# mLSTM heads of a hybrid decoder layer: chunks of 256 tokens with three carried states instead of 512 with one, and lone diagonal blocks as unsplit fp32 products

## The chip, the core and the metric

The kernel runs on one core of a Trainium2 chip. The core has a matrix engine (TensorE, PE in the profile, with its weight loads PEld), a vector engine (VectorE, DVE), an activation engine (ScalarE, ACT), a general engine (GpSimd, POOL) and a queue engine that issues most of the transfers (SyncE, SP). Matmuls write to eight accumulation banks of 128 x 512 fp32 (PSUM); everything else lives in on-chip memory (SBUF) of 128 partitions or in device memory. The metric is device time in microseconds (us).

## The reference

One decoder layer on 1024 tokens of width 1024, all in fp32. After an RMSNorm one input projection feeds three groups: a matrix-memory LSTM (mLSTM, 4 heads of 256), dilated causal attention (8 heads of 64) and cross-attention into 256 memory tokens (4 heads of 128). Each group is gated, the outputs go through one output projection, and a last RMSNorm closes the layer. Only the mLSTM matters here. It is defined in chunks, with a state C, n and a running maximum m carried from chunk to chunk:

```python
bcum = jnp.cumsum(lf_c, axis=-1)
dlog = bcum[..., :, None] - bcum[..., None, :] + li_c[..., None, :]
dlog = jnp.where(causal, dlog, -jnp.inf)
a = bcum + m_prev[..., None]
m = jnp.maximum(a, jnp.max(dlog, axis=-1))
wts = jnp.exp(dlog - m[..., None]) * jnp.einsum('bhtd,bhsd->bhts', qt, kt)
inter = jnp.exp(a - m)
num = inter[..., None] * jnp.einsum('bhtd,bhde->bhte', qt, C) + \
    jnp.einsum('bhts,bhse->bhte', wts, vt)
den = inter * jnp.einsum('bhtd,bhd->bht', qt, n) + jnp.sum(wts, axis=-1)
h_out = num / jnp.maximum(jnp.abs(den), jnp.exp(-m))[..., None]
...
C = decay[..., None, None] * C + jnp.einsum('bhsd,bhse->bhde', g[..., None] * kt, vt)
n = decay[..., None] * n + jnp.einsum('bhs,bhsd->bhd', g, kt)
```

The result does not depend on the length of a chunk: a longer chunk has more products inside it (tokens against earlier tokens), a shorter one more products with the carried state and more state updates.

## The kernel before

Every fp32 matrix product is done as a sum of three products of a reduced type ("fp32r"). An operand x is split by the helper split (L81, L82) into a high part, copied by ScalarE, and a low part, the rest, which VectorE subtracts; then high x high, high x low and low x high are accumulated in one PSUM bank. A moving operand of this type is never given fewer than 256 columns, so a lone block of 128 is computed with a neighbour's columns that are not used. In one place, the attention's last block (L483), a lone block is instead multiplied as plain fp32, unsplit.

The work runs in stages: normalisation and first projections, cross-attention, dilated attention, the projections of the mLSTM input with its convolution (xm_block), the gates, and then the mLSTM heads. Weight blocks form one list, stream; fill(n) takes the next n pieces of it, until(name) goes on to a named block. A piece is a set of projection matmuls into one of two "pj" banks. These pieces are put between the steps of the heads: the numbers of HEAD_FILLS say how many. In the head stage they are the mLSTM's output gates (om) and three quarters of the output projection (out0 to out2); what is left runs after the last head. The last quarter, "last", multiplies the second half of the mLSTM output, normalises and stores.

The program text does not fix the order of instructions on an engine. A scheduler of the compiler sets it: it takes ready instructions by their place in the text, by its own estimate of times. Once set, each engine goes through its list strictly in order.

gates() (from L616) makes, on four partitions (one per head) and 1024 tokens, the running maximum mm, the sums of the log forget gates t0 (restarted at each chunk, L643) and from them uu = t0 - mm. It stacks four rows in stk: li - t0 (row 0), the weight of a key in the state at the chunk's end (row 32), the weight of the carried state for a query (row 64) and exp(-m) (row 96). Eight transposes (L656) turn them into columns, gcol. uu goes to device memory as u_d, from where each head reads its row into all partitions.

A unit is (h, c): head h, half c of 512 tokens, which before is one chunk. There are 8, in order, each with four blocks of 128 tokens. For a unit run, with fills between:
- head_weights: reads the row ub (L669), adds the causal mask to its diagonal blocks (ud, L671), splits the input, projects the queries (L686 to L688, the key projection is folded into them), and for each key block s makes the products with all queries from s on (L704 to L706), exps (L709, L711), the weighted product (L712) and its split. A bank of "s1" (three) holds the scores.
- head_values: for c = 0 it first sums the state over all four blocks: transposes (L731), weighted keys (L734, L735), products with the values into two "s1" banks (L739 to L741), split into ch and cl. Then for each query block b: for c = 1 the product with the state (L757 to L759), scaled on ScalarE (L761) into ci; the weighted values over the key blocks up to b (L766 to L768) into the one "po" bank; then normalisation sums (L771 to L776).
- head_out: denominators, head norm, gate and store of the unit before.

Tiles are named by tags, and a tag has a fixed number of buffers: "g" 13, "x4" 3 (the split values vh and vl take two), "t2k" 4, P0 to P7 and sw0, sw1 one each. A tile with a taken tag waits until the earlier one is read for the last time.

Of the kernel before, what the change touches and what calls it, by code (L numbers as in the profile page):

```python
# [20 lines left out]
P = 128  # L21
# [7 lines left out]
def hymba_kernel(ctx: ExitStack, tc: tile.TileContext, x, xt, memt, chv, w_all, w_out,  # L29
# [23 lines left out]
    def s1():  # L53
        return pst("s1", 3)
# [22 lines left out]
    def dram(name, shape):  # L77
        return dr.tile(shape, F32, name=name, tag=name)
# [534 lines left out]
    u_d = dram("u_d", [4, T])  # L613
    late = {}

    def gates():  # L616
# [32 lines left out]
        S.activation(stk[32:36, 0:512], stk[0:4, 0:512], AF.Exp, bias=uu[:, 511:512])  # L649
        S.activation(stk[64:68, 512:1024], uu[:, 512:1024], AF.Exp, bias=mm[:, 511:512])  # L650
        S.activation(stk[96:100, :], mm, AF.Exp, scale=-1.0)
        nc.sync.dma_start(u_d, uu)
        for half in range(2):
            o = tp()
            for i in range(4):
                PE.transpose(o[:, i * P:(i + 1) * P], stk[:, (4 * half + i) * P:(4 * half + i + 1) * P], ident)  # L656
            V.tensor_copy(gcol[:, 4 * half:4 * half + 4, :, :],
                          o.rearrange("p (s q c) -> p s q c", s=4, q=4)[:, :, :, 0:4])
# [4 lines left out]
    def head_weights(u):  # L663
# [17 lines left out]
        xh, xl, qh, ql = [g4(F32R).rearrange("p (d t) -> p d t", d=2) for _ in range(4)]  # L681
        for d in range(2):
            split(xh[:, d, :], xl[:, d, :], xc[2 * h + d][:, cs])
        for d in range(2):
# [4 lines left out]
            split(qh[:, d, :], ql[:, d, :], o)  # L689
        vh, vl = x4([P, 4, 258], F32R), x4([P, 4, 258], F32R)  # L690
# [4 lines left out]
        for s in range(4):  # L695
            n = (4 - s) * P
            sg = 4 * c + s
            o = s1()
            ss = slice(s * P, (s + 1) * P)
            t0 = min(s, 2) * P  # L700
            w0 = s * P - t0
            wd = 512 - t0
            for d in range(2):
                PE.matmul(o[:, :wd], xh[:, d, ss], qh[:, d, t0:], start=d == 0, stop=False)  # L704
                PE.matmul(o[:, :wd], xh[:, d, ss], ql[:, d, t0:], start=False, stop=False)
                PE.matmul(o[:, :wd], xl[:, d, ss], qh[:, d, t0:], start=False, stop=d == 1)  # L706
            e = t2k()
            bias = gcol[:, sg, 0, h:h + 1]
            S.activation(e[:, :P], ud[:, s, :], AF.Exp, bias=bias)  # L709
            if n > P:  # L710
                S.activation(e[:, P:n], ub[:, (s + 1) * P:512], AF.Exp, bias=bias)  # L711
            V.tensor_tensor(e[:, :n], o[:, w0:w0 + n], e[:, :n], op=MUL)  # L712
            wh = tagged(("pth", "P3", "P1", "P0")[s], [P, n], F32R, 2 if s == 0 else 1)
            wl = tagged(("ptl", "P2", "sw0", "sw1")[s], [P, n], F32R, 2 if s == 0 else 1)
            split(wh, wl, e[:, :n])
            wts.append((wh, wl))
        return qh, ql, vh, vl, wts

    def head_values(u, parts):
# [5 lines left out]
        nc.sync.dma_start(gt, om_d[h][c])  # L725
        if c == 0:
            cps = [s1(), s1()]
            for s in range(4):
                o = tp()
                for d in range(2):  # L730
                    PE.transpose(o[:, d * P:(d + 1) * P], xc[2 * h + d][:, s * P:(s + 1) * P], ident)  # L731
                gs = gcol[:, s, 1, h:h + 1]
                xg = tagged("P4" if s % 2 == 0 else "P7", [P, 2, 256], F32R)
                S.activation(xg[:, 0, :], o[:, :256], AF.Copy, scale=gs)  # L734
                V.scalar_tensor_tensor(xg[:, 1, :], o[:, :256], gs, xg[:, 0, :].bitcast(F32), op0=MUL, op1=SUB)  # L735
                for d in range(2):
                    od = cps[d][:, :258]
                    dsl = slice(d * P, (d + 1) * P)
                    PE.matmul(od, xg[:, 0, dsl], vh[:, s, :], start=s == 0, stop=False)  # L739
                    PE.matmul(od, xg[:, 0, dsl], vl[:, s, :], start=False, stop=False)  # L740
                    PE.matmul(od, xg[:, 1, dsl], vh[:, s, :], start=False, stop=s == 3)  # L741
            ch = tagged("P5", [P, 2, 258], F32R)
            cl = tagged("P6", [P, 2, 258], F32R)
            for d in range(2):
                split(ch[:, d, :], cl[:, d, :], cps[d][:, :258])
            cst["c", h] = (ch, cl)
# [3 lines left out]
        for b in range(4):  # L750
            bs = slice(b * P, (b + 1) * P)
            ci = None
            if c == 1:
# [6 lines left out]
                ci = tagged("P4" if b % 2 == 0 else "P7", [P, 258])  # L760
                S.activation(ci, o[:, :258], AF.Copy, scale=gcol[:, 4 + b, 2, h:h + 1])  # L761
            o = po()
            for s in range(b + 1):
                wh, wl = wts[s]
                w0 = (b - s) * P
                PE.matmul(o[:, :258], wh[:, w0:w0 + P], vh[:, s, :], start=s == 0, stop=False)  # L766
# [9 lines left out]
            V.bn_aggr(mv[:, b, :], st6[:, b, :])  # L776
        return gt, dens, mv
# [389 lines left out]
```

## Time and profile before

| what | value |
|---|---|
| median of 3 runs | 1048.72 us (1047.23 to 1049.53) |
| the profiled execution | 1047.84 us |
| its span in the profile | 1046.0 us |
| granted TensorE clock, mean | 0.997 of full |
| TensorE busy in the first 600 us | 591.85 us |
| TensorE busy from 690 to 985 us | 292.3 us |
| TensorE busy in the last 61 us | 51.58 us |

The profile page lists for each engine the time in which it had an instruction at work. TensorE's matmuls overlap one another, so its busy time tells whether it stood idle, and the distance between the starts of two matmuls tells what one costs. A row of a group reads: line, engine, operation, tile written and tiles read, shapes, count, then busy time and the mean of one in ns, then the engine's idle time just before, with what ended it. A row of the waits reads: who waited, for whom, total us, times, longest us. A row of the time order reads: start, duration, engine, line, operation, tiles, shapes, count.

### The profile page before, as it was taken

The page shows a single profiled execution, that of the slowest core. Times are in us where ns is not written, and L with a number is a line of the kernel's source. Part 1 is how long each engine was busy: PE and PEld are TensorE (multiplying, and loading weights), DVE is VectorE, ACT ScalarE, POOL GpSimd, SP SyncE. Part 2 cuts the span into 40 slices and gives each one's busy share as a digit, 9 for nine tenths or more (in the row PEclk, how much of TensorE's full clock was granted, in tenths as well). Part 3 has the DMA queues.
Part 4 walks back from the last instruction along what each step waited for, and adds up shares of the span by engine and source line. Part 5 has one row for each costly group of instructions (what it writes and reads, how often), then busy time and mean ns, then how long its engine had stood idle before and what let it go on. Part 6 is the DMA issues. An engine that isn't in the chain of part 4 may idle for free.

```text
span 1046.0 us, 17249 instructions
## 1 busy us (share of the span) xinstructions
PE 1022.9 (98%) x6512; PEld 915.4 (88%) x6512; DVE 684.5 (65%) x1459; ACT 447.7 (43%) x884; POOL 293.9 (28%) x305
## 2 busy tenths in 40 slices
PE   9999999999999999999999999999999999999996
PEld 6888888988889888778888879899999999999996
DVE  8475555537687777875558886835568786774375
ACT  3543533325565555654324454534445344330221
POOL 1440212346611344601000011412044243121352
PEclk9999999999999999999999999999999999999998
DMA  9832222232201131322124344535389446333322
GB/s 332 271 110 99 84 84 85 75 88 74 60 27 55 47 73 39 76 68 61 71 71 126 107 132 142 140 102 152 112 276 290 136 125 188 105 122 122 107 113 84
DMA packets 75283, 121.09 MB, mean 116 GB/s; under 512 B 6460, under 2 KB 45884, under 8 KB 75200
## 3 DMA queue, kind: packets, MB, share of 16 engines
q1 hardware_dynamic: 60736, 105.83, 31.1%
q0 software_dynamic: 14464, 14.16, 6.2%
q8 instruction: 51, 0.84, 0.3%
q14 instruction: 32, 0.26, 0.1%
HBM read 83.22 MB, written 31.51 MB: 110 GB/s over the span
## 4 chain that ended last, share of the span: by engine, by line
PE 74%; DMA 9%; DVE 8%; issue 3%; ACT 2%; POOL 2%; SPq 0%; POOLq 0%; ACTq 0%; DVEq 0%
PE pj L167 11%; PE pj L168 11%; PE pj L169 11%; PE pj L178 4%; PE pj L179 4%; PE pj L177 4%; PE pj L211 3%; PE pj L212 3%; PE pj L213 3%; PE tp L478 3%; DMA wr<-in_w_out_dram 2%; DMA wr<-y 2%; PE s L453 2%; PE po L487 1%; PE s L454 1%
## 5 line engine op out<-in xcount | busy, mean ns | idle before, releaser
L167 PE MATMUL pj<-hn,wh 128*128 128x512 f32 x544 | 216.7, 398 | 3.3 <-DVE t2k L290 1.4
L169 PE MATMUL pj<-hn,wl 128*128 128x512 f32 x544 | 217.2, 400 | 0.0
L168 PE MATMUL pj<-hn,wh 128*128 128x512 f32 x544 | 216.2, 397 | 0.0
L167 PEld LDWEIGHTS pj<-hn,wh 128*128 128x128 f32 x544 | 102.3, 188 | 26.7 <-ACT t2k L383 1.7
L81 ACT ACTIVATE wh<-wr 128x1024 fp32r<-128x1024 f32 x67 | 70.8, 1058 | 127.3 <-PE pj L168 55.7
L169 PEld LDWEIGHTS pj<-hn,wl 128*128 128x128 f32 x544 | 102.2, 188 | 22.6
L168 PEld LDWEIGHTS pj<-hn,wh 128*128 128x128 f32 x544 | 102.3, 188 | 22.4
L211 PE MATMUL pj<-wh,hn 128*128 128x256 f32 x384 | 108.0, 281 | 0.5 <-ACT st L261 0.5
L213 PE MATMUL pj<-wh,hn 128*128 128x256 f32 x384 | 107.4, 280 | 0.0
L212 PE MATMUL pj<-wl,hn 128*128 128x256 f32 x384 | 107.3, 279 | 0.0
L82 POOL TENSOR_TENSOR wl<-wr,wh 128x1024 fp32r<-128x1024 f32 x23 | 55.8, 2426 | 137.9 <-ACT wh L81 98.9
L82 DVE TENSOR_TENSOR wl<-wr,wh 128x1024 fp32r<-128x1024 f32 x44 | 58.1, 1319 | 49.3 <-ACT wh L81 38.4
L81 ACT ACTIVATE pth<-tp 128x512 fp32r<-128x512 f32 (+2 forms) x96 | 50.2, 540 | 73.6 <-PE tp L478 42.5
L82 DVE TENSOR_TENSOR ptl<-tp,pth 128x512 fp32r<-128x512 f32 (+2 forms) x96 | 58.0, 618 | 28.6 <-ACT pth L81 28.2
L211 PEld LDWEIGHTS pj<-wh,hn 128*128 128x128 f32 x384 | 72.1, 188 | 1.4 <-ACT st L261 0.8
L212 PEld LDWEIGHTS pj<-wl,hn 128*128 128x128 f32 x384 | 72.1, 188 | 0.4
L213 PEld LDWEIGHTS pj<-wh,hn 128*128 128x128 f32 x384 | 72.0, 188 | 0.2
L177 PE MATMUL pj<-wh,hn 128*128 128x256 f32 x256 | 71.9, 281 | 0.0
L179 PE MATMUL pj<-wh,hn 128*128 128x256 f32 x256 | 71.6, 280 | 0.0
L178 PE MATMUL pj<-wl,hn 128*128 128x256 f32 x256 | 71.6, 280 | 0.0
L461 ACT ACTIVATE P<-P,mx 128x128 f32<-128x128 f32 (+3 forms) x64 | 49.3, 772 | 21.0 <-DVE mx L457 20.7
L851 DVE TENSOR_TENSOR hn<-pj,hn 128x512 f32<-128x512 f32 x48 | 32.9, 687 | 35.5 <-PE pj L179 35.4
(324 smaller groups left out, 2633.7 us busy)
## 6 DMA issues: line engine op xcount, KB each, us to landing
wr<-in_w_all_dram SPq DMA_DIRECT2D x54, 512.0 KB
x<-v POOLq DMA_DIRECT2D x16, 512.0 KB, 5.4
wr<-in_w_out_dram SPq DMA_DIRECT2D x16, 512.0 KB
wr<-y SPq DMA_DIRECT2D x16, 512.0 KB
y<-t2k SPq DMA_DIRECT2D x24, 256.0 KB
v<-P SPq DMA_DIRECT2D x24, 256.0 KB
zm<-st SPq DMA_DIRECT2D x16, 256.0 KB
g<-g POOLq DMA_DIRECT2D x32, 128.0 KB, 2.7
```

What stands on the lines that cost most here:

```text
L81: S.activation(hi, src, AF.Copy)
L82: (eng_lo or V).tensor_tensor(lo, src, hi.bitcast(F32), op=SUB)
L167: PE.matmul(o, hi[:, ks], ah(k, cs), start=k == 0, stop=False)
L168: PE.matmul(o, hi[:, ks], al(k, cs), start=False, stop=False)
L169: PE.matmul(o, lo[:, ks], ah(k, cs), start=False, stop=k == KC - 1)
L177: PE.matmul(o, ah(k, cs), hi[:, ks], start=k == 0, stop=False)
L178: PE.matmul(o, ah(k, cs), lo[:, ks], start=False, stop=False)
L179: PE.matmul(o, al(k, cs), hi[:, ks], start=False, stop=k == nk - 1)
L211: PE.matmul(oi, hn_h(4 * kh + k, cs), hi[:, ks], start=kh == 0 and k == 0 and i == 0, stop=False)
L212: PE.matmul(oi, hn_h(4 * kh + k, cs), lo[:, ks], start=False, stop=False)
L213: PE.matmul(oi, hn_l(4 * kh + k, cs), hi[:, ks], start=False, stop=kh == 1 and k == 3 and i == 1)
L461: S.activation(pr, pr, AF.Exp, bias=mx, scale=-1.0, accum_out=ls)
```

## The change

The head's text goes from one chunk of 512 tokens to two of 256, so that a head has four chunks and three carried states (after chunks 0, 1 and 2); units, fills and the order of calls stay.

- gates: sums restart every 256 tokens; key weights and state weights are made for three chunk ends. Two decay factors (state weight at the last token of chunks 1 and 2) go by two small transfers each through device memory into all partitions.
- head_weights: for each of the two chunks in the half, the first key block is multiplied with both query blocks (256 columns) in split form. The second key block against its own query block is the lone diagonal one: it is multiplied as unsplit fp32, from xc and from a copy qf of the queries in fp32, which ScalarE makes from the bank. One bank holds both, one product and one split of 384 columns follow.
- state_sums and state_done: the state work is cut out into two functions, over two blocks per chunk. The full state is kept in fp32 (cf, tag P6), multiplied by the decay and added to by VectorE, and split into ch and cl (P4, P5).
- head_values: for c = 0 state 0 is made first and used for blocks 2 and 3, and state 1 is made at the end. For c = 1 the sums of state 2 are made first, blocks 0 and 1 use state 1, state 2 is finished ahead of block 2. Weighted values run over the key blocks of the chunk alone.

```diff
+    dec_d = [dram(f"dec{c}", [1, 4]) for c in range(2)]
...
-        for c in range(2):
-            cs = slice(c * 512, c * 512 + 512)
-            V.tensor_tensor_scan(t0[:, cs], one1.broadcast_to([4, 512]), ff[:, cs], 0.0, op0=MUL, op1=ADD)
+        for c in range(4):
+            cs = slice(c * 256, c * 256 + 256)
+            V.tensor_tensor_scan(t0[:, cs], one1.broadcast_to([4, 256]), ff[:, cs], 0.0, op0=MUL, op1=ADD)
...
-        S.activation(stk[32:36, 0:512], stk[0:4, 0:512], AF.Exp, bias=uu[:, 511:512])
-        S.activation(stk[64:68, 512:1024], uu[:, 512:1024], AF.Exp, bias=mm[:, 511:512])
+        for c in range(3):
+            cs, e = slice(c * 256, c * 256 + 256), c * 256 + 255
+            S.activation(stk[64:68, e + 1:e + 257], uu[:, e + 1:e + 257], AF.Exp, bias=mm[:, e:e + 1])
+            S.activation(stk[32:36, cs], stk[0:4, cs], AF.Exp, bias=uu[:, e:e + 1])
         S.activation(stk[96:100, :], mm, AF.Exp, scale=-1.0)
         nc.sync.dma_start(u_d, uu)
+        for c in range(2):
+            late["dec", c] = tagged("mx", [P, 4], F32, 2)
+            nc.sync.dma_start(dec_d[c].rearrange("o h -> h o"), stk[64:68, c * 256 + 511:c * 256 + 512])
+            nc.sync.dma_start(late["dec", c], dec_d[c].broadcast_to([P, 4]))
...
+        qf = tagged("sw1", [P, 2, 2, P])
...
             split(qh[:, d, :], ql[:, d, :], o)
+            S.activation(qf[:, d, :, :], o.rearrange("p (a b t) -> p a b t", a=2, b=2)[:, :, 1, :], AF.Copy)
...
-        for s in range(4):
...
+        for a in range(2):
+            sg = 4 * c + 2 * a
+            x0 = c * 512
+            s0, s1_ = slice(2 * a * P, (2 * a + 1) * P), slice((2 * a + 1) * P, (2 * a + 2) * P)
+            both = slice(2 * a * P, (2 * a + 2) * P)
             o = s1()
             for d in range(2):
-                PE.matmul(o[:, :wd], xh[:, d, ss], qh[:, d, t0:], start=d == 0, stop=False)
-                PE.matmul(o[:, :wd], xh[:, d, ss], ql[:, d, t0:], start=False, stop=False)
-                PE.matmul(o[:, :wd], xl[:, d, ss], qh[:, d, t0:], start=False, stop=d == 1)
+                PE.matmul(o[:, :256], xh[:, d, s0], qh[:, d, both], start=d == 0, stop=False)
+                PE.matmul(o[:, :256], xh[:, d, s0], ql[:, d, both], start=False, stop=False)
+                PE.matmul(o[:, :256], xl[:, d, s0], qh[:, d, both], start=False, stop=d == 1)
+            for d in range(2):
+                PE.matmul(o[:, 256:384], xc[2 * h + d][:, x0 + s1_.start:x0 + s1_.stop], qf[:, d, a, :],
+                          start=d == 0, stop=d == 1)
             e = t2k()
+            S.activation(e[:, :P], ud[:, 2 * a, :], AF.Exp, bias=gcol[:, sg, 0, h:h + 1])
+            S.activation(e[:, P:256], ub[:, s1_], AF.Exp, bias=gcol[:, sg, 0, h:h + 1])
+            S.activation(e[:, 256:384], ud[:, 2 * a + 1, :], AF.Exp, bias=gcol[:, sg + 1, 0, h:h + 1])
+            V.tensor_tensor(e[:, :384], o[:, :384], e[:, :384], op=MUL)
+            wh = tagged(("pth", "P2")[a], [P, 384], F32R, 2 - a)
+            wl = tagged(("ptl", "sw0")[a], [P, 384], F32R, 2 - a)
+            split(wh, wl, e[:, :384])
...
+    def state_sums(h, cc, vh, vl):
+        gcol = late["gcol"]
+        cps = [s1(), s1()]
+        for i in range(2):
...
+            xg = tagged("P3" if i == 0 else "P7", [P, 2, 256], F32R)
...
+    def state_done(h, cc, cps):
+        if cc == 0:
+            cst["f", h] = tagged("P6", [P, 2, 258])
+        cf = cst["f", h]
+        ch = tagged("P4", [P, 2, 258], F32R)
+        cl = tagged("P5", [P, 2, 258], F32R)
+        for d in range(2):
+            if cc == 0:
+                S.activation(cf[:, d, :], cps[d][:, :258], AF.Copy)
+            else:
+                V.scalar_tensor_tensor(cf[:, d, :], cf[:, d, :], late["dec", cc - 1][:, h:h + 1], cps[d][:, :258],
+                                       op0=MUL, op1=ADD)
+            split(ch[:, d, :], cl[:, d, :], cps[d][:, :258] if cc == 0 else cf[:, d, :])
...
         if c == 0:
+            state_done(h, 0, state_sums(h, 0, vh, vl))
+        else:
+            late_state = state_sums(h, 2, vh, vl)
...
         for b in range(4):
...
-            if c == 1:
+            a = b // 2
+            if b == 2 and late_state is not None:
+                state_done(h, 2, late_state)
+            if 2 * c + a > 0:
...
-                ci = tagged("P4" if b % 2 == 0 else "P7", [P, 258])
+                ci = tagged("P3" if b % 2 == 0 else "P7", [P, 258])
...
-            for s in range(b + 1):
+            for s in range(2 * a, b + 1):
...
+        if c == 0:
+            state_done(h, 1, state_sums(h, 1, vh, vl))
         return gt, dens, mv
```

More of the change, by code (lines that the diff above doesn't have):

```diff
@@ L716, in head_weights @@
+            S.activation(e[:, P:256], ub[:, s1_], AF.Exp, bias=gcol[:, sg, 0, h:h + 1])
[4 more added lines that the diff above has]
+            split(wh, wl, e[:, :384])
             wts.append((wh, wl))
         return qh, ql, vh, vl, wts
+    def state_sums(h, cc, vh, vl):
+        gcol = late["gcol"]
+        cps = [s1(), s1()]
+        for i in range(2):
+            sg = 2 * cc + i
+            s = sg % 4
+            o = tp()
+            for d in range(2):
+                PE.transpose(o[:, d * P:(d + 1) * P], xc[2 * h + d][:, sg * P:(sg + 1) * P], ident)
+            gs = gcol[:, sg, 1, h:h + 1]
+            xg = tagged("P3" if i == 0 else "P7", [P, 2, 256], F32R)
+            S.activation(xg[:, 0, :], o[:, :256], AF.Copy, scale=gs)
+            V.scalar_tensor_tensor(xg[:, 1, :], o[:, :256], gs, xg[:, 0, :].bitcast(F32), op0=MUL, op1=SUB)
+            for d in range(2):
+                od = cps[d][:, :258]
+                dsl = slice(d * P, (d + 1) * P)
+                PE.matmul(od, xg[:, 0, dsl], vh[:, s, :], start=i == 0, stop=False)
+                PE.matmul(od, xg[:, 0, dsl], vl[:, s, :], start=False, stop=False)
+                PE.matmul(od, xg[:, 1, dsl], vh[:, s, :], start=False, stop=i == 1)
+        return cps
@@ new lines, in state_done @@
+    def state_done(h, cc, cps):
[4 more added lines that the diff above has]
+        cl = tagged("P5", [P, 2, 258], F32R)
+        for d in range(2):
+            if cc == 0:
[4 more added lines that the diff above has]
+            split(ch[:, d, :], cl[:, d, :], cps[d][:, :258] if cc == 0 else cf[:, d, :])
+        cst["c", h] = (ch, cl)
@@ L725, in head_values @@
         nc.sync.dma_start(gt, om_d[h][c])
+        late_state = None
         if c == 0:
[L727 to L746, printed above, removed]
+            state_done(h, 0, state_sums(h, 0, vh, vl))
+        else:
+            late_state = state_sums(h, 2, vh, vl)
         dens = tagged("dens", [P, 4], F32, 2)
@@ L759, in head_values @@
                     PE.matmul(o[:, :258], ql[:, d, bs], ch[:, d, :], start=False, stop=d == 1)
[L760 to L761 removed]
+                ci = tagged("P3" if b % 2 == 0 else "P7", [P, 258])
+                S.activation(ci, o[:, :258], AF.Copy, scale=gcol[:, 4 * c + b, 2, h:h + 1])
             o = po()
[L763 to L766 removed]
+            wh, wl = wts[a]
+            for s in range(2 * a, b + 1):
+                w0 = (b - s) * P if s == 2 * a else 256
+                PE.matmul(o[:, :258], wh[:, w0:w0 + P], vh[:, s, :], start=s == 2 * a, stop=False)
                 PE.matmul(o[:, :258], wh[:, w0:w0 + P], vl[:, s, :], start=False, stop=False)
```

14 lines of the change are left out of this document (removed).

## The prediction

> **What bounds the kernel now.** I read the page first, then the stretches, then TensorE's waits, then single instructions in order of time.
>
> ```profile
> span 1046.0 us, 17249 instructions
> PE 1022.9 (98%) x6512; PEld 915.4 (88%) x6512; DVE 684.5 (65%) x1459; ACT 447.7 (43%) x884; POOL 293.9 (28%) x305
> PE 74%; DMA 9%; DVE 8%; issue 3%; ACT 2%; POOL 2%; SPq 0%; POOLq 0%; ACTq 0%; DVEq 0%
> ```
>
> TensorE (PE) is busy for 98% of the span and makes up 74% of the chain that ended last. A share over the whole span can hide a slack stage, so the second view cuts out the mLSTM heads (about 678 to 950 us) and what follows them. Columns: span, then busy time and count for PE, weight loads, DVE, ACT, POOL, then granted clock, DMA share, GB/s.
>
> ```profile
> 690.00:730.00 40.00, 39.45 (x318) 38.42 (x317) 16.91 (x51) 17.29 (x39) 7.68 (x11) 1.00 0.41 116
> 770.00:810.00 40.00, 39.35 (x311) 38.15 (x309) 28.11 (x63) 20.65 (x40) 16.46 (x14) 1.00 0.91 292
> 890.00:930.00 40.00, 40.00 (x326) 39.41 (x325) 30.89 (x78) 13.36 (x27) 5.56 (x6) 1.00 0.37 119
> PE s L704 <- DVE t2k L712: 1.2, 1, 1.2
> PE po L767 <- DMA x<-v: 1.1, 1, 1.1
> PE tp L656 <- ACT g L649: 0.8, 1, 0.8
> PE tp L757 <- ACT P L761: 0.4, 2, 0.2
> ```
>
> PE is 98 to 100% busy in these stretches, at full clock, and the waits (the last four rows, from 640 us on) are about 1 us each. DVE is second with 31 of 40 us, ACT has half its time free. So the head stage is bound by the number and width of matmuls, and the sum is made in PE time. A matmul's "busy" time overlaps the next one's; what it costs is the distance between starts:
>
> ```profile
> 709.40 0.40 PE L687 MATMUL pj<-g,wvg 128*128 128x512 f32 x1
> 709.63 0.40 PE L688 MATMUL pj<-g,wvg 128*128 128x512 f32 x1
> ...
> 718.72 0.28 PE L768 MATMUL po<-x,sw 128*128 128x258 f32 x1
> 718.84 0.33 PE L704 MATMUL s<-g,g 128*128 128x384 f32 x1
> 719.01 0.33 PE L705 MATMUL s<-g,g 128*128 128x384 f32 x1
> ...
> 719.88 0.28 PE L704 MATMUL s<-g,g 128*128 128x256 f32 x1
> 720.00 0.28 PE L705 MATMUL s<-g,g 128*128 128x256 f32 x1
> ...
> 312.90 0.60 PE L478 MATMUL tp<-ident,P 128*128 128x128 f32 x4
> 313.34 0.39 PE L483 MATMUL po<-pth,g 128*128 128x128 f32 x2
> 313.56 0.49 PE L478 MATMUL tp<-ident,P 128*128 128x128 f32 x3
> ```
>
> So: 512 columns 0.233 us, 384 columns 0.175, 256 and 258 columns 0.12. Four transposes take 313.34 - 312.90 = 0.44, that is 0.11 each. L483 is the one place where this kernel already does a lone 128x128 block as an unsplit fp32 product: it stands as two records and takes 313.56 - 313.34 = 0.22.
>
> **The change part by part, on PE.** A unit is one head's half of 512 tokens; there are 8, and 4 heads.
> - Scores. Removed per unit: 6 matmuls each of 512, 384, 256 and 256 columns, 6 x (0.233 + 0.175 + 0.12 + 0.12) = 3.89 us. Added: for each of two chunks 6 of 256 columns (0.72) and two fp32 products (0.44), 2.32 us. Saves 1.57, over 8 units 12.6 us. The fp32 product is the cheaper form for a lone block: 0.44 against 6 x 0.12 = 0.72 for the split form, whose moving operand is kept at 256 columns. Its price comes from L483, the same operation and shape.
> - Weighted values. Block pairs fall from 10 to 6 per unit, three 258-column matmuls each: 12 x 0.12 = 1.44, over 8 units 11.5 us saved.
> - Products with the carried state. From 4 blocks per head to 6, six matmuls each: 12 x 0.12 = 1.44, over 4 heads 5.8 us added.
> - State sums. From 4 blocks of 128 tokens per head to 6, each two transposes and six matmuls: 2 x (0.22 + 0.72) = 1.88, over 4 heads 7.5 us added.
>
> Sum on PE: -12.6 - 11.5 + 5.8 + 7.5 = **-10.8 us**.
>
> One rule of the Trainium skill stands against my price for the fp32 product. The page "TensorE: Matmul & The Clock Gate", section "Back-to-back issue gap", gives about 81 ns per matmul for a sustained stream at 128 columns; by it the 64 added fp32 records would be 64 x 0.03 = 1.9 us cheaper in all. The rows at 313 us give 0.11 per record and not 0.08, so the measured number stands.
>
> **On the other engines.**
>
> ```profile
> L82 DVE TENSOR_TENSOR ptl<-t2k,pth 128x512 fp32r<-128x512 f32 x7 | 6.0, 856 | 1.4 <-ACT pth L81 1.4
> L712 DVE TENSOR_TENSOR t2k<-s,t2k 128x512 f32<-128x512 f32 x7 | 4.8, 688 | 1.5 <-PE s L706 1.5
> L712 DVE TENSOR_TENSOR t2k<-s,t2k 128x384 f32<-128x384 f32 x7 | 3.9, 552 | 0.4 <-PE s L706 0.4
> L82 DVE TENSOR_TENSOR P<-t2k,P 128x384 fp32r<-128x384 f32 x7 | 3.8, 547 | 0.7 <-ACT P L81 0.7
> L735 DVE SCALAR_TENSOR_TENSOR P<-tp,tg,P 128x256 fp32r<-128x256 f32 x14 | 6.5, 477 | 2.9 <-ACT P L734 2.9
> L82 DVE TENSOR_TENSOR P<-s,P 128x258 fp32r<-128x258 f32 x8 | 3.2, 420 | 3.6 <-ACT P L81 3.6
> L771 DVE TENSOR_TENSOR P<-po,P 128x258 f32<-128x258 f32 x14 | 5.9, 423 | 8.9 <-PE po L768 6.8 <-ACT P L761 2.1
> L734 ACT ACTIVATE P<-tp,tg 128x256 fp32r<-128x256 f32 x14 | 6.3, 470 | 11.3 <-PE tp L731 11.3
> L81 ACT ACTIVATE P<-s 128x258 fp32r<-128x258 f32 x8 | 2.7, 378 | 5.7 <-PE s L741 5.7
> ```
>
> DVE loses, per unit, score products and low halves of 512, 256 and 128 columns and gains one pair of 384. The 384 pair is 1.10 us and the 512 pair 1.54; by width the 256 and 128 pairs are at most as dear as the 384 pair, I take 0.8 and 0.6. That is -1.54 - 0.8 - 0.6 + 1.10 = -1.84, over 8 units -15 us. Per head it gains 2 x 0.477 (weighted keys), 4 x 0.420 (low halves of two more states), 4 x 0.42 to 0.55 (the new recurrence: no row shows this form; the ends are the 258-column add and the 384 product, I take 0.45, near the same width) and 2 x 0.423: about 5.3, over 4 heads +21 us. Net about +6 us on an engine that has 23% free even in the last stretch above. ACT gains two copies of 256 columns per unit (0.47 each, by L734) and ten operations of about 0.4 per head, and loses one exp per unit and the wide copies; at 17 busy us in 40 that is covered. None of this is on PE's path while PE has other ready work.
>
> Two things are. First, the **gates**: four ACT exps and two scans more, on four rows.
>
> ```profile
> 672.86 0.72 ACT L649 ACTIVATE g<-g,P 4x512 f32<-4x512 f32 x1 [0.41 <-DVE g L648]
> ```
>
> ACT's exps stand between the scans and the transposes L656, for which PE already waits 0.8 us. Four more at this row's 0.72 would be 2.9 us and bound the delay from above, nothing bounds it from below; they have half the width, and the two old ones shrink as well. I take **+1.0 us** (0 if PE is given filling work there). Second, the **state handoff**: in each unit the state is made (ACT 0.38, then DVE 0.42, twice) and used in the same head_values call, in a single buffer that the last product must first have left. Before, it was made in one unit and used in the next. The view of time shows what PE does meanwhile:
>
> ```profile
> 716.71 0.39 PE L705 MATMUL s<-g,g 128*128 128x512 f32 x1
> ...
> 717.28 0.28 PE L212 MATMUL pj<-wl,hn 128*128 128x256 f32 x1
> 717.39 0.28 PE L766 MATMUL po<-x,pth 128*128 128x258 f32 x1
> ```
>
> Scores of the next unit (L705), projection pieces (L212) and values (L766) alternate, so a handoff of about 1.2 us can be filled. I charge 0.2 us to each of the 8 handoffs inside a unit, by the two 0.2 us waits of L757 on L761: **+1.6 us**. Bounds: 0, and 1.2 x 8 = 9.6.
>
> Two tiny DMA pairs on SP carry the two decay factors to all partitions. SP waits for each write to land before its read, and behind it stand the row load of head 0 and projection weights.
>
> ```profile
> 675.02 0.32 SPq L270 DMA_DIRECT2D zm<-st  x1
> 680.58 0.32 SPq L803 DMA_DIRECT2D zs<-zm  x1
> 681.00 0.39 SPq L669 DMA_DIRECT2D t2k<-u_d  x1
> ```
>
> SP already stands from 675.0 to 680.6 us for another landing, ahead of the row load of head 0 (the third row); I cost the pairs at nothing because they can land in that same time. Without that cover they cost up to one more such gap, 5 to 6 us.
>
> Sum against the profiled execution, 1047.84 us: 1047.84 - 10.8 + 1.0 + 1.6 = 1039.6. That execution lies 0.88 below the median of the three runs (1048.72), so on the median the forecast is **1040.5 us**.
>
> **The rivals.**
> - Handoffs uncovered (slower). A state's whole turn is transpose to weighted keys, 0.47 + 0.48, then sums to halves, 0.38 + 0.42 + 0.42, and 0.45 for the recurrence in two cases of three: about 2.5 us. There are now 12 instead of 4, in series through each head, with the three PSUM banks of "s1" lent to them in every unit. If half of it lies open, 12 x 1.25 = 15, and the time is 1048.7 - 10.8 + 1 + 15 = 1054. It decides from (10.8 - 1.0) / 12 = 0.8 us per state on. Against it: the four turns of before left 0.4 us (L757). For it: nothing in before uses a state right after it is made.
> - Eviction late. If DVE's added 6 us falls where it is busiest (30.9 of 40 us between 890 and 930) and PE waits for it there: 1040.5 + 6 = 1046.5, 1045 with part of it covered.
> - SP's queue late by the decay pairs: 1040.5 + 5.5 = 1046.
> - The change doesn't do what it says: PE's stage is refilled at the pace of loads. Between 770 and 810 us the DMA share is 0.91; if this burst sets the pace, PE's saving turns into a wait there and the time stays at 1048 to 1049. Against it: PE is still 98% busy in that burst, and between 890 and 930 the share is down to 0.37.
>
> **How the numbers follow.** Forecast 0.54, with an own range of 1036 to 1045; eviction 0.14; SP 0.12; loads 0.07; handoffs uncovered 0.13. The low end, 1034.5, is the full 10.8 with the three waits of L704, L767 and L656 (3.1 us) gone too; the high end, 1050, takes in eviction, SP and loads and leaves out most of the uncovered handoffs. A measurement here can tell about 0.2% (2.1 us) from no change: faster than 1046.6 has 0.77 (forecast, most of eviction and SP), within 0.2% 0.09 (loads and edges), slower 0.14.
>
> **What would show it.** Right: scores at 12 matmuls of 256 columns and 8 fp32 records per unit, 16 fewer PE instructions in all (32 and 96 fewer in scores and values, 48 and 64 more for the states), PE still above 95% in the head stage, and the last output rows starting some 8 to 10 us earlier. Wrong: fp32 records further apart than 0.11; waits of products with the state (L757's successor) on ACT or DVE of several us in total; SP standing over 5 us at the decay reads; PE waiting on "x<-v" loads, since the last state sum of a first half now holds its value tiles to the end of the unit.

## The result, and the profile after

| | before | after |
|---|---|---|
| median, 7 runs each | 1049.51 us (1047.23 to 1052.3) | 1059.74 us (1054.2 to 1061.67) |
| ratio | 1 | 1.0085, 95% interval 1.0059 to 1.0112 |
| the profiled execution | 1047.84 us | 1059.74 us |
| its span | 1046.0 us | 1057.9 us |
| granted clock, mean | 0.997 | 0.987 |

One execution of e5_row_pool, further down, took 2020.5 us for a reason that is not known, and the median and ratio of that run go without it.

The changed kernel is slower by 0.6 to 1.1%; I had forecast 0.8% faster. The page of the changed kernel, its span and the busy times:

```profile
span 1057.9 us, 17285 instructions
PE 1024.0 (97%) x6496; PEld 917.0 (87%) x6496; DVE 693.5 (66%) x1477; ACT 455.4 (43%) x920; POOL 298.3 (28%) x305
```

Two things are to be seen. PE ran 16 instructions fewer, as counted in the prediction, yet was busy 1.1 us longer: its instructions took longer each. And the span less the busy time, in which PE stood idle, went from 1046.0 - 1022.9 = 23.1 to 1057.9 - 1024.0 = 33.9 us. The windows of the changed kernel (columns as in the prediction) say where:

```profile
0.00:600.00 600.00, 591.39 (x3178) 501.17 (x3179) 394.23 (x848) 277.95 (x577) 167.11 (x196) 1.00 0.31 94
690.00:730.00 40.00, 39.52 (x305) 38.80 (x306) 17.92 (x52) 18.76 (x45) 7.24 (x11) 0.93 0.33 102
770.00:810.00 40.00, 36.65 (x274) 35.16 (x273) 26.53 (x63) 18.64 (x39) 12.61 (x13) 0.91 0.79 260
890.00:930.00 40.00, 40.00 (x337) 39.69 (x336) 30.16 (x76) 13.72 (x31) 6.66 (x7) 1.00 0.35 106
```

The first 600 us are much as before (591.39 against 591.85 us busy). From 890 to 930 PE is full and at full clock, with 337 matmuls in 40 us where there were 326. In between the seventh number, the granted clock, falls to 0.93 and 0.91 where it was 1.00, and PE has lost 2.7 us of its busy time between 770 and 810. The longest of PE's waits from 640 us on:

```profile
PE s L715 <- ACT sw L698: 4.5, 1, 4.5
PE tp L791 <- ACT P L81: 2.9, 1, 2.9
PE pj L694 <- DVE hn L887: 2.4, 1, 2.4
PE s L711 <- ACT g L81: 2.2, 1, 2.2
```

Four single waits make 12.0 us; the four longest of before made 3.9. They stand at 690, 790, 882 and 821 us. Each is read below from the engine that PE waits for.

**At 690 us** PE waits for qf, the new fp32 copy of the queries. ACT, of the changed kernel, in order of time:

```profile
680.65 0.40 ACT L698 ACTIVATE sw<-pj 128x256 f32<-128x256 f32 x1
689.58 0.40 ACT L719 ACTIVATE t2k<-t2k,tg 128x128 f32<-128x128 f32 x1 [8.53 <-DMA t2k<-u_d]
689.89 0.36 ACT L698 ACTIVATE sw<-pj 128x256 f32<-128x256 f32 x1
```

The second copy takes 0.36 us, but it stands in ACT's list behind an exp (L719) that waits 8.53 us for the row load of head 0. PE's rows at that place:

```profile
685.39 0.39 PE L715 MATMUL s<-sw,g 128*128 128x128 f32 x2
690.31 0.80 PE L715 MATMUL s<-sw,g 128*128 128x128 f32 x2 [4.53 <-ACT sw L698]
...
693.67 0.41 PE L213 MATMUL pj<-wh,hn 128*128 128x256 f32 x1
693.89 0.41 PE L211 MATMUL pj<-wh,hn 128*128 128x256 f32 x1
...
695.36 0.28 PE L212 MATMUL pj<-wl,hn 128*128 128x256 f32 x1
695.48 0.28 PE L213 MATMUL pj<-wh,hn 128*128 128x256 f32 x1
```

A second loss is in the lower rows. After the wait, matmuls of 256 columns start 0.22 us apart, and only from 695 us on 0.12 again: PE runs at half its clock for 6.8 us, from 688.5 us, still inside the wait, to 695.3. PE worked in 5.0 us of that and lost half of it, 2.5 us, beside the 4.5 of the wait. Before, ACT had the same wait and PE did not. ACT's row of the kernel before:

```profile
685.58 0.62 ACT L711 ACTIVATE t2k<-t2k,tg 128x384 f32<-128x384 f32 x1 [5.90 <-DMA t2k<-u_d]
```

And PE's rows of the kernel before, at the same place:

```profile
686.60 0.28 PE L211 MATMUL pj<-wh,hn 128*128 128x256 f32 x1
688.08 0.39 PE L704 MATMUL s<-g,g 128*128 128x256 f32 x1 [1.20 <-DVE t2k L712]
```

There ACT stood 5.90 us behind the row load, but nothing that PE needed at once was behind it: scores and projection pieces ran until 686.6, and the wait then was 1.20 us. SP's rows of the changed kernel show why the landing came later too:

```profile
674.42 0.82 SPq L659 DMA_DIRECT2D mx<-dec  x2
676.51 0.32 SPq L270 DMA_DIRECT2D zm<-st  x1
684.38 0.32 SPq L839 DMA_DIRECT2D zs<-zm  x1
684.75 0.42 SPq L676 DMA_DIRECT2D t2k<-u_d  x1
```

From the store (L270) to the read that follows its landing (L839) SP stands 684.38 - 676.51 = 7.9 us, with the decay pairs just ahead (L659); before it was 680.58 - 675.02 = 5.6.

**At 790 us** PE's first product with the state (L791) waits for the state's copy. ACT there, in the changed kernel, where L718 to L720 are exps of the scores, L759 and L81 the state's copies:

```profile
786.80 0.40 ACT L718 ACTIVATE t2k<-t2k,tg 128x128 f32<-128x128 f32 x1 [1.95 <-DMA y<-t2k]
...
788.28 0.40 ACT L718 ACTIVATE t2k<-t2k,tg 128x128 f32<-128x128 f32 x1 [0.49 <-DMA y<-t2k]
...
789.78 0.36 ACT L759 ACTIVATE P<-s 128x258 f32<-128x258 f32 x1
790.05 0.37 ACT L81 ACTIVATE P<-s 128x258 fp32r<-128x258 f32 x1
```

The copy takes 0.36 us and stands behind six exps, which waited for a store to leave a "t2k" buffer, and one operation of head_out (L841, at 789.17). At 821 us the split of the queries stands behind exps of the same kind.

**What it adds up to.** A stretch at half clock began near the end of each of these waits: 6.8, 6.8, 3.4 and 3.4 us long at 688, 791, 822 and 883 us. One more of 3.4 us stands at 9 us, after a wait of 2.3 us in the first projections. Before there was one only after the last matmul, where it costs nothing. Half of the time in such a stretch in which PE worked is lost. With that, the span is taken apart (PE idle is counted up to the last matmul, 8.6 us before the end in both; work is busy time less what the clock lost):

| us | span | PE idle | lost to half clock | work at full clock |
|---|---|---|---|---|
| before | 1046.0 | 14.5 | 0 | 1022.9 |
| after | 1057.9 | 25.3 | 10.8 | 1013.2 |
| difference | +11.9 | +10.8 | +10.8 | -9.7 |

The work went down by 9.7 us where the prediction had summed 10.8. It was paid back twice: once as waits, once as the half clock behind them. Not all of that is the change's: the wait at 7 us and the 1.7 us lost at 9 us lie ahead of the changed text, and similar waits there come in some executions and not in others. From 640 us on, idle time went from 5.6 to 16.2 us and 9.1 us were lost to half clock. The work column is good to about 2 us: the runs e2 to e12 below have the same matmuls as the changed kernel and show 1013.2 to 1015.6. The timed runs show the clock's part as well: span x (1 - granted clock) has a median of 11.6 us over the 7 runs of the changed kernel and of 4.2 over 23 runs of before (which includes the end, after the last matmul).

### The profile page after: what moved, and what is told of

The parts are those of the page before. It is cut to its first block, busy times and chain, and to the rows that moved or that the text cites. A ratio compares the mean times of both kernels' runs of the same rounds, so it can differ in the third digit from the quotient of the medians.

```text
span 1057.9 us, 17285 instructions
## 1 busy us (share of the span) xinstructions
PE 1024.0 (97%) x6496; PEld 917.0 (87%) x6496; DVE 693.5 (66%) x1477; ACT 455.4 (43%) x920; POOL 298.3 (28%) x305
## 4 chain that ended last, share of the span: by engine, by line
PE 76%; DVE 10%; DMA 7%; ACT 3%; issue 2%; POOL 1%; SPq 0%; POOLq 0%; ACTq 0%; DVEq 0%
PE pj L167 10%; PE pj L168 10%; PE pj L169 10%; PE pj L177 4%; PE pj L178 4%; PE pj L179 4%; PE pj L211 4%; PE pj L213 4%; PE pj L212 3%; PE tp L478 3%; DVE t2k L580 2%; PE s L453 2%; PE po L487 1%; PE s L454 1%; PE po L486 1%
## 5 line engine op out<-in xcount | busy, mean ns | idle before, releaser
L81 ACT ACTIVATE wh<-wr 128x1024 fp32r<-128x1024 f32 x67 | 70.8, 1058 | 121.5 <-PE pj L168 56.3
L169 PEld LDWEIGHTS pj<-hn,wl 128*128 128x128 f32 x544 | 102.2, 188 | 23.7 <-POOL wl L82 1.1
L82 POOL TENSOR_TENSOR wl<-wr,wh 128x1024 fp32r<-128x1024 f32 x23 | 57.3, 2490 | 132.6 <-ACT wh L81 86.2
L82 DVE TENSOR_TENSOR wl<-wr,wh 128x1024 fp32r<-128x1024 f32 x44 | 58.3, 1325 | 40.9 <-ACT wh L81 40.7
L81 ACT ACTIVATE pth<-tp 128x512 fp32r<-128x512 f32 (+2 forms) x96 | 50.2, 540 | 72.9 <-PE tp L478 42.6
L82 DVE TENSOR_TENSOR ptl<-tp,pth 128x512 fp32r<-128x512 f32 (+2 forms) x96 | 58.0, 618 | 28.4 <-ACT pth L81 28.0
L467 POOL TENSOR_SCALAR P<-P,ls 128x128 f32<-128x128 f32 (+4 forms) x40 | 29.7, 747 | 88.9 <-DVE ls L462 59.6
```

Of the source, the lines that this page charges most:

```text
L81: S.activation(hi, src, AF.Copy)
L82: (eng_lo or V).tensor_tensor(lo, src, hi.bitcast(F32), op=SUB)
L169: PE.matmul(o, lo[:, ks], ah(k, cs), start=False, stop=k == KC - 1)
```

## The experiments

My theory after this result, the queue theory: the time is lost where an operand that PE needs at once stands in ACT's or DVE's strict order behind an instruction that waits for a transfer. Rivals: the decay pairs make the row load late, and that alone is the cause (decay theory); a state is used right after it is made and its own chain of copies lies open, the prediction's rival (handoff theory); the fp32 blocks themselves are dear; and the waits only shift, so that whatever is mended turns up elsewhere (shifting theory). All results in one table; ratios are against runs of before on the same chip (e8 to e10 ran on another chip than the other experiments), and the three columns at the right are of the one profiled execution.

| run | median, runs | ratio, interval | PE idle | half clock | work |
|---|---|---|---|---|---|
| e1_split_diag | 1062.8, 4 | 1.0115 (1.0083 to 1.0147) | 28.8 | 3.6 | 1018.8 |
| e2_qf_dve | 1058.8, 6 | 1.0085 (1.0058 to 1.0112) | 26.2 | 6.3 | 1014.5 |
| e3_store_from_zs | 1058.74, 4 | 1.0078 (1.0048 to 1.0108) | 28.5 | 5.9 | 1015.6 |
| e4_dec_pool | 1058.89, 5 | 1.0084 (1.0055 to 1.0112) | 25.2 | 7.3 | 1013.2 |
| e5_row_pool | 1053.19, 9 | 1.0034 (1.0018 to 1.005) | 23.1 | 8.2 | 1014.7 |
| e6_state0_early | 1055.0, 5 | 1.0048 (1.0027 to 1.007) | 26.5 | 4.0 | 1015.3 |
| e7_both | 1049.91, 12 | 1.001 (0.9994 to 1.0027) | 22.3 | 5.1 | 1015.1 |
| e8_states_early | 1050.09, 12 | 1.0003 (0.9988 to 1.0019) | 20.6 | 3.3 | 1015.1 |
| e9_qf_pool | 1054.47, 6 | 1.0049 (1.003 to 1.0067) | 25.9 | 5.8 | 1013.3 |
| e10_all | 1048.9, 12 | 0.9998 (0.998 to 1.0015) | 20.9 | 3.4 | 1013.8 |
| e11_all_store_zs | 1050.41, 10 | 1.0015 (1.0001 to 1.0029) | 26.0 | 3.4 | 1014.4 |
| e12_states_early_qf_dve | 1054.55, 12 | 1.0049 (1.0031 to 1.0067) | 23.7 | 3.2 | 1013.7 |

**e1_split_diag** takes the fp32 blocks back to split products and drops qf:

```diff
-            S.activation(qf[:, d, :, :], o.rearrange(...)[:, :, 1, :], AF.Copy)
...
-                PE.matmul(o[:, 256:384], xc[2 * h + d][:, x0 + s1_.start:x0 + s1_.stop], qf[:, d, a, :],
-                          start=d == 0, stop=d == 1)
+                PE.matmul(o[:, 256:], xh[:, d, s1_], qh[:, d, both], start=d == 0, stop=False)
+                PE.matmul(o[:, 256:], xh[:, d, s1_], ql[:, d, both], start=False, stop=False)
+                PE.matmul(o[:, 256:], xl[:, d, s1_], qh[:, d, both], start=False, stop=d == 1)
...
```

> The changed kernel with the lone diagonal blocks back in split form (six matmuls of 256 columns each), and so without the fp32 copy qf of the queries. Three theories for the 10 us that the changed kernel is slower. Queue theory: TensorE does save its 10.8 us, but operands that it needs at once are copied by ScalarE, whose queue is in order, behind exps that wait for a transfer to land; each such wait of over 2 us also brings one or two stretches of 3.4 us at half clock. Here it expects the 4.5 us wait at 690 us (fp32 scores for qf) and its 6.8 us at half clock (3.4 us of work) to go, against 16 x (0.72 - 0.44) = 4.5 us more matmul work: 1055 to 1057. Handoff theory (the rival of the prediction: state made and used at once, uncovered): the state chain is the same, so only the added work shows, 1064. Decay theory (the small transfers of the decay factors make SP's queue and the row load of head 0 late): TensorE waits at the same place for the weighted scores instead, 1062 to 1064.

Measured: 1062.8 us, a miss of the queue theory in this form. Its longest waits:

```profile
PE pj L211 <- ACT st L261: 6.5, 1, 6.5
PE tp L791 <- ACT P L81: 4.4, 2, 3.9
```

qf is gone, and PE now waits 6.5 us for L261, an eviction of a projection bank. ACT has that behind the exps of the next half, the first of which waits for the mask addition to that half's own row:

```profile
687.34 0.41 ACT L718 ACTIVATE t2k<-t2k,tg 128x128 f32<-128x128 f32 x1 [8.63 <-DMA t2k<-u_d]
695.44 0.40 ACT L717 ACTIVATE t2k<-t2k,tg 128x128 f32<-128x128 f32 x1 [3.33 <-POOL t2k L678]
```

So taking the copy away moves the wait to the next thing that ACT has behind a row load. The work column answers the other question: 1018.8 - 1013.2 = 5.6 us more without the fp32 blocks. With the 2 us by which that column varies, this part of the change is a gain of about the size that was priced, 16 x (0.72 - 0.44) = 4.5.

**e2_qf_dve** makes qf on VectorE instead:

```diff
-            S.activation(qf[:, d, :, :], o.rearrange(...)[:, :, 1, :], AF.Copy)
+            V.tensor_copy(qf[:, d, :, :], o.rearrange(...)[:, :, 1, :])
```

> The changed kernel with the copy qf made by VectorE instead of ScalarE; nothing else. Queue theory: qf no longer stands behind the exp that waits for the row load, so the 4.5 us wait at 690 us and its half clock go, 1051 to 1053; the waits at 790 and 821 us stay if the order stays. Handoff theory: no change, 1058 to 1061. Decay theory: the row load is as late as before, TensorE stands a little further on for as long, 1058 to 1060.

Measured: 1058.8 us, a miss as well: no better than the change itself, and the same lesson as e1. The long wait for qf is gone, and the same eviction from ACT takes its place:

```profile
PE pj L211 <- ACT st L261: 4.0, 1, 4.0
PE tp L844 <- DVE g L835: 3.9, 3, 2.0
```

**e3_store_from_zs** writes the gated output over another tile before its store, so that the "t2k" buffer needn't wait for the store:

```diff
-            V.tensor_tensor(sx, sx, zt, op=MUL)
-            nc.sync.dma_start(y_d[2 + j // 4][c][:, j % 4, :], sx)
+            V.tensor_tensor(zt, sx, zt, op=MUL)
+            nc.sync.dma_start(y_d[2 + j // 4][c][:, j % 4, :], zt)
```

> The changed kernel with the last product of the head output written into the gate tile (zs) and stored from there, so that the t2k buffers come free when VectorE has read them and not when the store has landed; the exps of the next unit no longer wait for a store. Queue theory: the waits at 790 us (state copy behind those exps, 2.9) and 821 us (query split behind them, 2.2) go with their 6.8 and 3.4 us at half clock, 10 us less or, if gate loads now come late, 5: 1050 to 1055. Handoff theory: the state's own chain of copies is untouched, 1058 to 1061. Decay theory: no change, 1058 to 1061.

Measured: 1058.74 us, a miss; up to here the handoff and the decay theory had forecast the times better than the queue theory. The exps no longer wait for the store, but the compiler's order put another waiting instruction ahead of the state's copy:

```profile
788.80 1.06 ACT L81 ACTIVATE hn<-wr 128x1024 fp32r<-128x1024 f32 x1 [5.38 <-DMA wr<-y]
789.76 0.37 ACT L759 ACTIVATE P<-s 128x258 f32<-128x258 f32 x1
```

**e4_dec_pool** issues the four transfers of the decay pairs from GpSimd instead of SP:

```diff
-            nc.sync.dma_start(dec_d[c]...)
-            nc.sync.dma_start(late["dec", c], ...)
+            G.dma_start(dec_d[c]...)
+            G.dma_start(late["dec", c], ...)
```

> The changed kernel with the four small transfers of the decay factors issued from GpSimd's queue instead of SP's. Decay theory: the gate store behind which the row load of head 0 stands lands in 5.5 us again instead of 7.9, the wait at 690 us falls below 2 us and brings no half clock, 1052 to 1054. Queue theory: the row load comes up to 2 us earlier, so the wait at 690 us shrinks to 2 to 4 us but stays, as do those at 790, 821 and 882: 1055 to 1060. Handoff theory: 1058 to 1061.

Measured: 1058.89 us, so the decay pairs by themselves are not the cause. SP's rows of this run:

```profile
673.80 0.32 SPq L270 DMA_DIRECT2D zm<-st  x1
679.61 0.32 SPq L839 DMA_DIRECT2D zs<-zm  x1
680.02 0.38 SPq L676 DMA_DIRECT2D t2k<-u_d  x1
```

And PE's two longest waits of this run:

```profile
PE pj L211 <- ACT sw L698: 5.1, 1, 5.1
PE tp L791 <- ACT P L81: 2.8, 1, 2.8
```

SP's stand is back at 679.61 - 673.80 = 5.8 us, about the 5.6 of before, and the row load is issued 4.7 us earlier than in the changed kernel. PE still waits 5.1 us for the copy qf, more than the 2 to 4 that the queue theory gave it: PE stands there from 680.1 us on, where it was 685.8 in the changed kernel. The pairs make SP's stand some 2 us longer; the wait is there without them.

**e5_row_pool** leaves ACT's list as it is and makes what it waits for earlier: the first row load goes by GpSimd's queue, past SP's stand.

```diff
-        nc.sync.dma_start(ub, u_d[h:h + 1, cs].broadcast_to([P, 512]))
+        (G if u == (0, 0) else nc.sync).dma_start(ub, u_d[h:h + 1, cs].broadcast_to([P, 512]))
```

> The changed kernel with one transfer moved: the row load of head 0's first half (u_d into all partitions) is issued from GpSimd's queue, not from SP's, where it stands behind a gate store. In the changed kernel and in e2, e3, e4 TensorE waits 4.1 to 5.1 us near 690 us, each time for something that ScalarE does after the exp that waits for this load. Queue theory: the load comes some 5 us earlier, the wait near 690 us falls to under 1.5 us and brings no half clock, 4 + 3 us less than the changed kernel: 1051 to 1054. Shifting theory (TensorE has too little other work at this point since the change took out 1.6 us of scores and 1.4 us of values per unit, and stands at the next operand instead): the wait goes to another line near 700 us with half or more of its length, 1056 to 1059. Handoff theory (own turn of the states is what costs): 1057 to 1060.

Measured: 1053.19 us, inside the queue theory's range. ACT's row of this run:

```profile
681.99 0.40 ACT L719 ACTIVATE t2k<-t2k,tg 128x128 f32<-128x128 f32 x1 [3.63 <-DMA t2k<-u_d]
```

And PE's two longest waits of this run:

```profile
PE tp L791 <- ACT P L81: 2.8, 1, 2.8
PE pj L694 <- DVE hn L887: 2.4, 1, 2.4
```

The exp runs 689.58 - 681.99 = 7.6 us earlier and the wait for qf is gone, while those at 790 and 882 us stay as they were. The median is 1059.74 - 1053.19 = 6.6 us lower for one transfer on another queue. The profiled execution shows less of it, since at 1056.66 us it was among the longest: idle time fell by 2.2 us (part of the 4.5 came back as a wait of 2.1 for L261, the eviction of e1 and e2, with 3.4 us at half clock behind it) and the loss to the clock by 2.6, of which 1.7 is the stretch at 9 us that this execution didn't have.

**e6_state0_early** moves the state of the first chunk ahead of the filling pieces, from the start of head_values to the end of head_weights:

```diff
+        if c == 0:
+            state_done(h, 0, state_sums(h, 0, vh, vl))
         return qh, ql, vh, vl, wts
...
-        if c == 0:
-            state_done(h, 0, state_sums(h, 0, vh, vl))
-        else:
+        if c == 1:
             late_state = state_sums(h, 2, vh, vl)
```

> The changed kernel with state 0 of each head made at the end of head_weights, ahead of the filling projection pieces, instead of at the start of head_values where it is used two blocks later. Queue theory, as it stands after e3 (the state copy waits in ScalarE's queue behind a split that waits for a load, 2.8 to 4.3 us at 790 us in every run): the wait at 790 us goes with its half clock, 3 + 2 to 3 us less: 1053 to 1055; the one at 690 stays. Handoff theory in its own form (about 1 us for each state, by its own chain of copies): a third of the states are covered now, 4 us less, but spread over four places, not at 790 alone. Shifting theory: 1057 to 1060.

Measured: 1055.0 us. The 2.9 us at the state product are gone; the wait for qf remains:

```profile
PE s L715 <- ACT sw L698: 4.8, 1, 4.8
PE pj L177 <- ACT sw L698: 2.6, 2, 1.8
PE s L749 <- DVE P L743: 2.5, 3, 1.6
```

Its gain is in the clock: idle time is no less than the changed kernel's (26.5 against 25.3), as several waits of under 2 us stand where the one of 2.9 was, but the loss to the clock fell from 10.8 to 4.0 (from 9.1 to 4.0 from 640 us on). The time alone doesn't tell the queue theory from the handoff theory, whose 4 us fit as well, and this run's interval touches that of the changed kernel. The traces tell them apart: the handoff theory put the loss in four places, and the changed kernel waits for a copied state (L791 on L81) at 790 us alone.

**e7_both** is e5 and e6 together.

> Both moves of e5 and e6 in one kernel. Queue theory: both waits and their half clock go, 11 to 13 us less than the changed kernel, so at or a little below the kernel before: 1046 to 1050. Shifting theory: 1055 to 1059. Handoff theory: 1055.

Measured: 1049.91 us, ratio 1.001 (0.9994 to 1.0027). The two gains add, within the noise: 6.6 + 4.7 = 11.3 from 1059.74 give 1048.4. So the theory that the waits only shift is wrong for these two, and they explain the loss against before. They don't explain why the forecast gain of 8 us is missing: e7's profiled execution still has 22.3 - 14.5 = 7.8 us more idle time than before and 5.1 us at half clock. What is left are waits of under 2 us:

```profile
PE pj L177 <- ACT sw L698: 2.9, 2, 1.7
PE s L749 <- DVE P L743: 2.8, 3, 1.6
```

The last five runs look for a version that beats both. **e8_states_early** is e7 with the sums of state 2 moved in the same way:

```diff
-        late_state = None
-        if c == 1:
-            late_state = state_sums(h, 2, vh, vl)
...
+        return qh, ql, vh, vl, wts, (state_sums(h, 2, vh, vl) if c == 1 else None)
```

> e7 with the sums of state 2 moved to the end of head_weights as well, so that of the three state sums of a head two lie ahead of the filling pieces. e7's trace still has waits of TensorE for weighted keys (1.6 us at 807, the first operand of state 2's sums) and for the last low half of a state (1.8 at 942), the first and the last with a stretch of half clock. Queue theory: the wait at 807 goes with its half clock, 1.6 + 1.7 us less, the one at 942 stays: 1046 to 1049. Shifting theory (what is left is the same idle time in another place): 1049 to 1051.

Measured: 1050.09 us, as e7 and as the shifting theory gave it. **e9_qf_pool** is e7 with qf made on GpSimd, as the sum of the two halves of the split:

```diff
-            S.activation(qf[:, d, :, :], o.rearrange(...)[:, :, 1, :], AF.Copy)
+            G.tensor_tensor(qf[:, d, :, :], *[q[:, d, :].rearrange(...)[:, :, 1, :].bitcast(F32) for q in (qh, ql)], op=ADD)
```

> e7 with the copy qf made on GpSimd as the sum of the two halves qh and ql, which stand in SBUF, so that a projection bank no longer waits for ScalarE's copy to come free. e7's trace has two waits of TensorE for that copy (1.7 us at 784, 1.2 at 906, the second with a stretch of half clock), and the copies are 7 us of ScalarE. Queue theory: both go, unless GpSimd, which also makes 2.4 us splits in order, brings qf later than ScalarE did: 1045 to 1048. Shifting theory: 1049 to 1051, with waits for GpSimd at the fp32 scores.

Measured: 1054.47 us, 4.6 us worse than e7 and outside both ranges. Its longest waits are of other kinds, evictions on DVE (L806), the low half of a state (L82) and a load of values:

```profile
PE po L801 <- DVE P L806: 3.2, 3, 1.8
PE tp L793 <- DVE P L82: 3.2, 1, 3.2
PE po L802 <- DMA x<-v: 1.9, 1, 1.9
```

**e10_all** has the edits of e8 and e9 together.

> All four moves together: row load of head 0 on GpSimd's queue, states 0 and 2 summed ahead of the filling pieces, qf made on GpSimd. TensorE's work at full clock in e7 is 1015 us, 8 us less than before the change; idle time 22.3 against 14.5. Queue theory: idle time falls to 15 to 18 and half clock in the head stage to one stretch at most: 1041 to 1046, faster than the kernel before. Shifting theory: 1048 to 1051.

Measured: 1048.9 us, ratio 0.9998 (0.998 to 1.0015): level with before. **e11_all_store_zs** adds the edit of e3 to it.

> e10 and e3 together: the exps of a unit no longer wait in ScalarE's queue for the store of an earlier unit to land. Queue theory: in e10 TensorE still stands idle 20.9 us, 6.4 more than in the kernel before, and part of that is behind ScalarE and the product of head_out; 2 to 4 us less, 1045 to 1047. Shifting theory: 1048 to 1050.

Measured: 1050.41 us, no gain. **e12_states_early_qf_dve** is e8 with qf on VectorE as in e2.

> e8 with the copy qf on VectorE instead of ScalarE (e10 has it on GpSimd). Queue theory: VectorE is the busier of the two (30 of 40 us against 14 to 20) and also in order, so the waits for a projection bank move from ScalarE's copy to VectorE's: 1048 to 1051, no better than e8. Shifting theory: the same, 1048 to 1051; this run tells whether the engine of the copy matters once the row load is early.

Measured: 1054.55 us, again outside both. In these five the queue theory's ranges held nowhere and the shifting theory's in e8 and e10: work stays at 1013 to 1015 us, and idle time at 21 to 26 us, in changing places. No version beats the kernel before. The profiled execution of e10 shows where its time is: its work is 1022.9 - 1013.8 = 9.1 us less than before, its idle time 6.4 more and its loss to the clock 3.4 more (half of it in a stretch at 10 us, ahead of the changed text), in all +0.7, and its span is 1046.8 against 1046.0.

## Why the prediction was wrong

- **The sum on PE held.** -10.8 forecast, -9.7 measured in the profiled execution, to within the 2 us of that column. The fp32 record is no dearer than L483's 0.11 us, as PE's rows of the changed kernel show, four records and the matmul after them: (729.25 - 728.89) / 4 = 0.09. 16 instructions fewer were forecast and counted. DVE gained 693.5 - 684.5 = 9.0 us where I had 6, ACT 455.4 - 447.7 = 7.7.

```profile
728.89 0.61 PE L715 MATMUL s<-sw,g 128*128 128x128 f32 x4
729.25 0.36 PE L211 MATMUL pj<-wh,hn 128*128 128x256 f32 x1
```

- **The range.** Its low end is 1034.8 us by its own terms and not 1034.5, which changes nothing.
- **The gates' +1.0 did not come.** PE's wait for the gate transposes, 0.8 us before, is not among the changed kernel's longer waits; in e6, e7 and e10 it is 0.9.
- **The step that failed first: "ACT has half its time free ... that is covered".** It is true of the busy share (17.29 of 40 us in the stretch from 690 before, 18.76 after) and says nothing of the order. ACT stood 8.53 us for a transfer, and each thing that I had added to ACT (qf, the state's copies) could come to stand behind it. e1 and e2 show that taking one operand out of ACT's list moves the wait to the next one, e5 that the late transfer is the lever: 6.6 us.
- **The handoffs, +1.6.** I priced them at 0.2 us each, by the two waits of L757 on L761, and that row was misread: L761 empties the bank that L757 writes, so it is no wait for a state. The kernel before has none of 0.2 us or more for a state from 640 us on. There a state was used one unit later than it was made, so that a unit's scores, pieces and values lay between; after the change that cover is gone for states 0 and 2. One handoff lay open for 2.9 us and, with the 6.8 us at half clock behind it, its removal is worth 4.7 (e6). The rival "handoffs uncovered" had the side and nearly the time right (1054), but not the mechanism: not 1.25 us at each of 12, but one long wait, most of it behind other work in ACT's list. That its time was near is luck.
- **The decay pairs, costed at nothing.** They made the landing ahead of the row load 2.3 us later, so nothing was too low; SP's stand at the decay reads themselves, named as a sign of being wrong, did not come. But e4 shows that the rival "SP's queue late" is not the cause by itself.
- **The price of a wait.** I counted waits at their own length. Here they cost more: from 640 us on, the changed kernel's waits of 1.1 us or more make 12.1 us, and 9.1 us were lost to half clock. Over the 13 traces after the change that loss is between 0.2 and 0.8 of such waits, so that a wait costs about 1.2 to 1.8 times its length. In all 14 traces of this study each wait of PE of 2.5 us or more had a stretch at half clock begin in it or within 1.5 us of its end; of those between 1.1 and 2.5 us some did. Shorter waits can add up: one stretch, at 9 us in e9, stands behind two of 0.6 and 0.8 us. In the 3.4 us ahead of each of the 36 stretches before the last matmul, PE's idle time sums to between 1.4 and 3.4 us. The Trainium skill has this as a rule, on the page "TensorE: Matmul & The Clock Gate", section "Why this matters for your kernels": no idle gaps above about 3 us between bursts of matmuls, or the clock falls back to half. The traces agree in kind, and go further down: 2.2 us were enough at 821 us. The prediction priced matmuls and did not ask what a new wait would do to the clock.

What stays open: the half clock was never changed by itself, so its cause is read from where it stands in 14 traces, behind waits, and not from an experiment. Each edit lets the scheduler set a new order, so a run differs from the changed kernel in more than its edit. The wait at 882 us was not taken away alone. More filling pieces in the heads were not tried. So for about half of the 19 us between forecast and measurement the step is shown (two late operands on ACT and their half clock, taken back in e7), and for the rest, the gain that stays away even in e7 and e10, the cause is open. That there is less PE work to cover the remaining waits with is a reason that fits, and only argued.

## What to carry to other kernels

On an engine that is busy for 98%, work that is taken out may also be cover that is taken out (argued here, not shown): list which waits ran beside it, and for each new operand which instruction stands ahead of it on its engine and what transfer that one waits for; the busy share doesn't tell. In this kernel it paid to make a carried state ahead of the filling work, not behind it, and to mend the late transfer rather than move one operand out of a blocked list. A new wait of TensorE of 2 us or more is to be priced above its length, here at up to 1.8 times.

## What the runs showed of the hardware

- Ahead of the last matmul, stretches at half clock come in multiples of 3.4 us, and they stand behind waits shorter than I knew of (1.1 to 2.5 us, sometimes, and once two that make 1.5 us together). In some kernels the spread of the times goes with them: e12 ran from 1047.19 to 1057.44 us over 12 runs, and the time in its runs goes with span x (1 - clock), which went from 2.1 to 9.5 us (correlation 0.91). It is 0.83 in e7, but 0.3 in e8 and in e10, so other things spread them too.
- The wait at 882 us stands behind two VectorE products of L846 that took 2.5 and 2.9 us, where the other 14 of that line took 0.7. VectorE's rows there, in the changed kernel:

```profile
876.60 5.31 DVE L846 TENSOR_TENSOR t2k<-t2k,zs 128x512 f32<-128x512 f32 x2
881.83 1.28 DVE L887 TENSOR_TENSOR hn<-pj,hn 128x512 f32<-128x512 f32 x2
```

And GpSimd's row at that time:

```profile
876.10 5.26 POOL L82 TENSOR_TENSOR hn<-wr,hn 128x1024 fp32r<-128x1024 f32 x2
```

Two products of two SBUF tiles take 5.31 us, beside two splits on GpSimd of 5.26, and PE's bank eviction (L887) stands behind them. The kernel before has such slow products too (up to 2.15 us at its L810), without a long wait of PE behind them. The Trainium skill, page "SBUF — State Buffer", section "SBUF: two separate sides", says that a VectorE operation with two SBUF inputs and a GpSimd operation share a pair of ports, which one of them holds for its whole instruction; these rows agree with it.
